# A two-layer decoder trunk on one Trainium2 core: identity transposes at the heads of groups left out, and the embedding input p laid out transposed by the host

## The chip, the core and the metric

The kernel runs on one core of a Trainium2 chip. The core has five engines, each with its own queue that it takes in order: TensorE (PE; its weight loads are listed as PEld), VectorE (DVE), ScalarE (ACT), GpSimd (POOL) and SyncE (SP), which here issues the DMAs. Engines wait for each other by semaphores. The metric is the device time of one launch in microseconds; three runs are known of the kernel before.

## The reference

The reference is a decoder trunk with two layers, on x of 256 rows and 1024 columns in float32. It computes, for layer i = 0, 1:

```
x = post_norm(x, 0.5 * swiglu(x, ffn1_w_in[i], ffn1_w_out[i]), ...)   # D_FF 2816
mix = fox_mixer(x, ...)  if i == 0  else  mla_mixer(x, ...)
x = post_norm(x, mix, ...)
x = post_norm(x, 0.5 * swiglu(x, ffn2_w_in[i], ffn2_w_out[i]), ...)
gate = sigmoid(x @ ple_w_gate[i] + ple_b_gate[i])
x = post_norm(x, gate * (p[i] @ ple_w_proj[i]), ...)                   # PLE_DIM 256
```

Here post_norm(x, d) is the layer norm of alpha * x + d. The FoX mixer is causal attention with 16 heads of 64 and a forget gate whose logarithms are summed along the sequence. The MLA mixer has 16 heads, a latent for the queries (384) and one for keys and values (256 + 64 rotary columns); the latter is computed once, from the x that leaves layer 0, by `kv_down`. p is an input of 2 x 1 x 256 x 256: a row of 256 for each layer and position.

## The kernel before

**Products.** Every matmul of the reference is computed as three products of operands that are split in a high and a low part: high x high, high x low, low x high (`mm3`, L608; `mm`, L615, records as L616). `parts` (L623) makes the two parts of an activation: ScalarE copies the source, rounded, to the high part (`high`, L629), and VectorE subtracts that from the source to get the low part (`low`, L633). x is held as two tiles of 128 rows, x0 and x1. `XT(t)` transposes one of them on TensorE, eight 128 x 128 blocks by a matmul with an identity (L620), into `xT`, in high and low parts.

**Weights.** A weight comes by a DMA of SP into one of three `raw` buffers, each 1 MB. ScalarE makes the high part of each half (L252, L260), VectorE the low part (L253, L264), into one of ten slots `hl0` to `hl9`, or into a tile that is free for the time (`fs`, `qk`, `ota`, `otb`, `gb`, `g4`). A raw buffer is loaded again when both its halves are split.

**The planner.** The class `Stream` decides at which point of the instruction stream a split is written. It keeps three model clocks while the kernel is built: one for TensorE (`pe_t`), one for ScalarE, one for VectorE. Each matmul adds to `pe_t` through `busy`, each transpose too:

```
def transpose(self, out, in_):
    self.nc.tensor.transpose(out, in_, self.ident)
    self.S.busy(pe=256)                                  # adds 116 ns to pe_t
...
if arrival <= self.pe_t + 500 and max(self.act_t, self.dve_t) <= self.pe_t + SLACK_NS:
```

`pump` (L384) is called after each group of products, and writes the next split when its load has arrived by the model and the two other clocks are no more than 1.6 us ahead of TensorE's. So what adds to `pe_t` decides ahead of which activation, norm or transposition a split stands in the queues of ScalarE and VectorE, and behind which a load on SP. The order of the splits among themselves is a written list (`ORDER`, and `FOX` in the mixer).

**The feed-forward network** (`ffn`, L721) runs over 11 chunks of 256 hidden columns. The first chunks are computed with the weights moving; the others in three groups, (2, 3, 4), (5, 6, 7), (8, 9, 10). At the head of each group, behind the first six matmuls of its first chunk, stands a `turn` on TensorE, which gets a free PSUM bank. In the first network of the program (`cold`) and in those that come before an embedding step (`ple`) the turns are:

- `T(0)` and `T(1)`: transposes of activations of the first chunks (not in the cold network);
- `spare` (L717): four transposes of the identity, whose result is not read;
- `ple_transpose` (L1033): four transposes of p, 128 x 128 each, and the parts of the result;
- `kv_transpose`: part of the key and value work, in the first network of layer 1.

**The embedding step** (`ple`, L1057) runs behind the second network of each layer. `ple_load` fetches p in the middle of that network (chunk 6), `ple_project` makes p @ Wp, and `ple` computes the gate with the slots of the weight `pg`: bias, eight weight tiles for x0, with `XT(1)` ahead of the seventh, then the same for x1 with `XT(0)` in that place, which transposes the normed x0 of the next layer. `post` is the sigmoid on ScalarE (L1080, with a table load ahead of the first), the product with the projection (L1081), the sum with x and its statistics (L689, L690); `ln_apply` is the norm (L698 to L705). Behind the boundary stand `kv_down`, whose weights are the four splits of 128 x 640, and the first chunk of the next network, whose silu is L783.

Of the kernel before, what the change touches and what calls it, by code (L numbers as in the profile page):

```python
# [510 lines left out]
class Trunk:  # L511
# [209 lines left out]
    def ffn(self, li, which, lni, kv=False, ple=False, at=None, cold=False, after=()):  # L721


        nc, S = self.nc, self.S
# [62 lines left out]
        def T(c):  # L787
            def f(tr):
                for t in range(2):
                    for kt in range(2):  # L790
                        self.transpose(
                            tr[:, 256 * kt + 128 * t : 256 * kt + 128 * t + 128],
                            g[c][:, 256 * t + 128 * kt : 256 * t + 128 * kt + 128],
                        )
                if c in summed:
                    gt = self.room(c, summed)
                    nc.scalar.activation(gt, tr, AF.Copy)
                    S.busy(act=512)
                    add(c)
                    return  # L800
                o = self.tl([128, 2, 512], F32R, "g4", 6)
                self.parts(o[:, 0, :], o[:, 1, :], tr)
                gT[c] = o

            return f

        def HT(c, gate, up, what=None):
            for half in range(2):
                ps = self.bank(*(up if half else gate))
                for u in range(2):  # L810
                    w = self.use(("wiu", li, which, c, 2 * half + u))
                    for kk, b in ((kk, b) for kk in range(4) for b in range(2)):
                        k = 4 * u + kk
                        if (half, k, b) == (0, 1, 0) and what:
                            what(self.bank(*up))
                        col = slice(256 * kk + 128 * b, 256 * kk + 128 * b + 128)
                        self.mm3(
                            ps[:, 256 * b : 256 * b + 256], lambda i: w[:, i, col], lambda i: self.xT[:, :, i, k, :],
                            (k, b) == (0, 0), (k, b) == (7, 1),
                        )  # L820
                if half == 0:
                    gt = self.room(c, summed)
                    nc.scalar.activation(gt, ps, AF.Silu)  # L823
                    S.busy(act=512)
            close(c, gt, ps)
# [14 lines left out]
        def add(c):  # L840

            tt, f = nc.vector.tensor_tensor, self.full[c]
            b = lambda i, n=1: f[:, 128 * i : 128 * (i + n)]
            tt(
                b(4, 2).rearrange("p (a b) -> p a b", b=128), b(0)[:, None, :].to_broadcast([128, 2, 128]),
                b(1, 2).rearrange("p (a b) -> p a b", b=128), op=ALU.subtract,
            )
            tt(b(6), b(5), b(1), op=ALU.subtract)
            tt(b(7), b(6), b(3), op=ALU.add)
            S.busy(dve=700)  # L850
            tag, o = self.home(homes)
            self.high(o[:, 0, :], f[:, 128:1024])
            S.between_sums()
            self.low(o[:, 0, :], o[:, 1, :], f[:, 128:1024])
            forms[c] = tag, o
# [93 lines left out]
        else:  # L949
# [14 lines left out]

        turns = (
            None if cold else T(0),
            self.spare if cold else T(1),
            self.kv_transpose if kv else self.ple_transpose if ple else self.spare,
        )
        x = self.turn["h"] if cold else 1 - self.turn["h"]  # L970
        for i, group in enumerate((((1,) + GROUPS[0]) if cold else GROUPS[0],) + GROUPS[1:]):
            for c in group:
                for f in at.get(c, ()):
                    f()
                if c == 2:
                    S.lend("gb")
                if c == 8:
                    S.reclaim("gb")
                if c == 10:
                    S.check("gb")  # L980
                    self.load_gb(li, lni)
                if c == 10 and kv:
                    self.kv_transpose_rope()
                if i == 0 and c == group[0]:
                    banks = ("tr", self.turn["tr"]), ("tr", 1 - self.turn["tr"])
                    turn = turns[0] and (lambda _: turns[0](self.bank("h", 1 - x)))
                    HT(c, *banks, turn)
                else:
                    HT(c, ("h", x), ("h", 1 - x), turns[i] if c == group[0] else None)
            if i < 2:  # L990
                if i == 1 and kv:
                    self.flush()
                sums([c for c in summed if (c < 5 and (cold or c != 1)) == (i == 0)], ("h", x))
                x = 1 - x
            if i == 1:
                S.lend(*after)
                combine()
# [26 lines left out]

    def ple_load(self, li):
        self.ple_p = self.tl([128, 512], F32, "g4", 6)
        for t in range(2):
            self.dma(
                self.ple_p[:, 256 * t : 256 * t + 256],
                None if self.rec else self.a["p"][li, 0, 128 * t : 128 * t + 128, :],  # L1030
            )

    def ple_transpose(self, tr):  # L1033
        nc = self.nc
        pt = self.ple_p
        for i in range(4):
            c = slice(128 * i, 128 * i + 128)
            self.transpose(tr[:, c], pt[:, c])
        self.ple_pT = self.tl([128, 2, 512], F32R, "g4", 6)
        self.parts(self.ple_pT[:, 0, :], self.ple_pT[:, 1, :], tr)  # L1040

    def ple_project(self, li):
        nc = self.nc
# [809 lines left out]
    Trunk(nc, (sb, ps), a, S, False, dr.tile([16, 256], F32, name="fox_c")).run()  # L1853


_INS = ["x", "p", "ln_g", "ln_b", "ple_b_gate", "fox_b_f", "mla_q_norm", "kv_norm"]


def _packed(np, a):

    def tiles(w, k):
        r, c = w.shape
        return w.reshape(r // (128 * k), k, 128, c).transpose(0, 2, 1, 3).reshape(r // (128 * k), 128, k * c)

    o = {}
    for n in ("ffn1", "ffn2"):
        w = a[n + "_w_in"].reshape(2, 2, 4, 128, 2, NCH, 256)
        o[n + "_in"] = w.transpose(0, 5, 1, 3, 2, 4, 6).reshape(2, NCH, 2, 128, 2048).copy()
        w = a[n + "_w_in"].reshape(2, 8, 128, 2, NCH, 256).transpose(0, 4, 3, 2, 1, 5).reshape(2, NCH, 2, 128, 2048)
        for li in range(2):  # L1870
            c = 1 if (n, li) == ("ffn1", 0) else 2
            o[n + "_in"][li, c:] = w[li, c:]
        o[n + "_out"] = np.stack([tiles(w, 2) for w in a[n + "_w_out"]])
    w = a["fox_w_in"][0]
    o["fq"], o["fk"] = (
        np.concatenate([tiles(w[:, c : c + 256], 8) for c in range(c0, c0 + 1024, 256)]) for c0 in (0, 1024)
    )
    o["fv"] = tiles(w[:, 2048:2560], 4)
    o["fvb"] = tiles(w[:, 2560:2816], 8)[0]
    o["fvc0"] = tiles(w[0:768, 2816:3088], 6)[0]  # L1880
    o["fvc1"] = tiles(w[768:1024, 2816:3088], 2)[0]
    o["fo"] = tiles(a["fox_w_o"][0], 2)
    o["mo"] = tiles(a["mla_w_o"][0], 2)
    o["pg"] = np.stack([tiles(w, 2) for w in a["ple_w_gate"]])
    o["pp"] = np.stack([tiles(w, 2) for w in a["ple_w_proj"]])
    o["kd"] = tiles(a["kv_w_down"], 4)
    o["dq"] = tiles(a["mla_w_dq"][0], 4)
    w = a["mla_w_uq"][0]
    r = w[:, :, 128:192].reshape(384, 1024)
    o["qr0"], o["qr1"] = tiles(r[0:256], 2)[0], tiles(r[256:384], 1)[0]  # L1890
    u = a["kv_w_up"]
    o["kvv"] = np.concatenate([tiles(u[:, h : h + 4, 128:256].reshape(256, 512), 2) for h in range(0, 16, 4)])
    n = np.concatenate([u[:, :, 0:128], w[:, :, 0:128]], 0)
    o["kq"] = np.concatenate([tiles(n[:, h : h + 2].reshape(640, 256), 5) for h in range(0, 16, 2)])
    t = a["x"][0].T.reshape(8, 128, 256)
    o["xt0"] = t[0:2]
    o["xt1"] = t[2:8].reshape(3, 2, 128, 256).transpose(0, 2, 1, 3).reshape(3, 128, 512)
    w = o["ffn1_in"][0, 0].reshape(2, 128, 4, 512).transpose(0, 2, 1, 3).reshape(8, 128, 512)
    o["w00"], o["w0"] = np.stack([w[0, :, 0:256], w[0, :, 256:512]]), w[1:8]
    return o  # L1900
# [34 lines left out]
```

## Time and profile before

| what | value |
|---|---|
| runs | 1050.86, 1048.7, 1050.29 us; median 1050.29 |
| profiled execution | 1049.6 us, span 1047.8 us, granted clock 0.998 |
| busy TensorE / weight loads | 1035.6 us (99%) / 948.6 us (91%) |
| busy VectorE / ScalarE / GpSimd | 891.8 us (85%) / 592.9 us (57%) / 58.0 us (6%) |
| DMA | 202.74 MB, mean 193 GB/s |

A row of a timeline gives the start in us from the span's start, the time from the first start to the last end of the instructions taken together, the engine, the line of the kernel, the operation, its output and inputs by the program's names, shapes, and the count; in square brackets the idle time of the engine before it and what ended that. A row of a group gives its summed busy time, the mean of one in ns, and idle time. The chain of waits is followed back from the last instruction of the program.

### The profile page before, as it was taken

Reading aid. Unit: us, or ns where it says so; the run is one execution under the profiler, and the core shown is the slowest. Engines: PE = TensorE matmul, PEld = TensorE weight load, DVE = VectorE, ACT = ScalarE, POOL = GpSimd, SP = SyncE. Lnnn points to the kernel's source line nnn. Section 1 sums busy time; section 2 is a strip of 40 time slices with the busy share of each in tenths; the row PEclk is TensorE's granted clock in tenths of the full one; section 3 lists DMA queues with packets and bytes.
Section 4 is the critical chain, followed back from the end, with each engine's and each line's share of the span. In section 5 each row is a group of like instructions: output and inputs, shape, how many; then the busy total and the mean of one; then the engine's idle time right before and its main releaser. Section 6 shows DMA issues by size and latency. Waiting matters only on the chain.

```text
span 1047.8 us, 17555 instructions
## 1 busy us (share of the span) xinstructions
PE 1035.6 (99%) x7085; PEld 948.6 (91%) x7085; DVE 891.8 (85%) x1312; ACT 592.9 (57%) x901; POOL 58.0 (6%) x88
## 2 busy tenths in 40 slices
PE   9999999999999999999999999999999999999996
PEld 8999898899889999998899898988999889898986
DVE  5788977868898979978979899888887989889877
ACT  6555563666755555663565646646776564646541
POOL 0000000122300000000220000000000000000000
PEclk9999999999999999999999999999999999999999
DMA  7855586455636363673674545743445564555732
GB/s 281 305 191 188 185 298 243 162 168 169 216 128 246 121 252 125 241 282 132 236 260 151 195 169 190 270 142 112 145 156 179 183 214 162 200 190 176 271 125 81
DMA packets 37476, 202.74 MB, mean 193 GB/s; under 512 B 3970, under 2 KB 9874, under 8 KB 16532
## 3 DMA queue, kind: packets, MB, share of 16 engines
q1 hardware_dynamic: 37396, 201.63, 54.3%
q8 instruction: 55, 0.90, 0.3%
q14 instruction: 25, 0.20, 0.1%
HBM read 200.55 MB, written 1.06 MB: 192 GB/s over the span
## 4 chain that ended last, share of the span: by engine, by line
PE 95%; DVE 2%; ACT 1%; issue 1%; DMA 0%; SPq 0%; DVEq 0%; ACTq 0%
PE h L616 53%; PE y L616 29%; PE tr L616 10%; PE tr L620 2%; DVE hl L253 1%; PE h L620 1%; DMA raw<-in_w_dram 0%; PE tr L1375 0%; DVE ts L300 0%; DVE x L705 0%; DVE tr L1720 0%; ACT qk L629 0%; DVE PT L633 0%; DVE ts L306 0%; DVE raw L308 0%
## 5 line engine op out<-in xcount | busy, mean ns | idle before, releaser
L616 PE MATMUL h<-xT,hl 128*128 128x256 f32 x3144 | 366.1, 277 | 1.2 <-ACT hl L327 0.7
L616 PEld LDWEIGHTS h<-xT,hl 128*128 128x128 f32 x3144 | 362.0, 188 | 2.9 <-ACT hl L327 1.2
L253 DVE TENSOR_TENSOR hl<-raw,hl 128x1024 fp32r<-128x1024 f32 (+5 forms) x271 | 314.2, 1190 | 36.1 <-ACT hl L252 35.0
L252 ACT ACTIVATE hl<-raw 128x1024 fp32r<-128x1024 f32 (+5 forms) x271 | 267.8, 1027 | 70.6 <-DVE raw L308 41.3
L616 PE MATMUL y<-hl,g 128*128 128x512 f32 x336 | 78.6, 391 | 0.0
L616 PEld LDWEIGHTS y<-hl,g 128*128 128x128 f32 x336 | 62.5, 188 | 12.6
L616 PE MATMUL h<-hl,xT 128*128 128x512 f32 (+2 forms) x312 | 67.9, 371 | 0.0
L616 PEld LDWEIGHTS h<-hl,xT 128*128 128x128 f32 x312 | 54.9, 188 | 9.8
L616 PE MATMUL y<-hl,otb 128*128 128x512 f32 x219 | 58.0, 399 | 0.0
L264 DVE TENSOR_TENSOR hl<-raw,hl 128x1024 fp32r<-128x1024 f32 (+2 forms) x44 | 52.3, 1192 | 0.8 <-ACT hl L260 0.7
L616 PE MATMUL y<-hl,xT 128*128 128x512 f32 (+3 forms) x282 | 52.7, 334 | 0.0
L260 ACT ACTIVATE hl<-raw 128x1024 fp32r<-128x1024 f32 (+2 forms) x44 | 45.2, 1029 | 9.7 <-DVE raw L308 9.1
L629 ACT ACTIVATE xT<-tr 128x512 fp32r<-128x512 f32 x28 | 16.1, 597 | 58.9 <-PE tr L620 58.9
L616 PEld LDWEIGHTS y<-hl,xT 128*128 128x128 f32 x282 | 44.1, 188 | 4.6 <-ACT xT L629 0.4
L616 PEld LDWEIGHTS y<-hl,otb 128*128 128x128 f32 x219 | 39.8, 188 | 8.4 <-DVE otb L633 0.3
L616 PE MATMUL y<-hl,ota 128*128 128x512 f32 x177 | 46.8, 398 | 0.1
L700 POOL TENSOR_TENSOR rs<-ve,mhalf 128x1 f32<-128x1 f32 x16 | 15.1, 942 | 519.8 <-DVE ve L699 519.8
L616 PE MATMUL tr<-xT,hl 128*128 128x256 f32 x360 | 42.5, 277 | 0.0
L616 PEld LDWEIGHTS tr<-xT,hl 128*128 128x128 f32 x360 | 41.7, 188 | 0.4
L616 PEld LDWEIGHTS y<-hl,ota 128*128 128x128 f32 x177 | 32.7, 189 | 7.7 <-DVE hl L253 0.6
L823 ACT ACTIVATE P<-h 128x512 f32<-128x512 f32 x33 | 19.7, 596 | 33.0 <-PE h L616 32.6
L300 DVE TENSOR_TENSOR ts<-raw 128x1024 f32<-128x1024 f32 x29 | 35.4, 1222 | 0.6
(322 smaller groups left out, 1632.7 us busy)
## 6 DMA issues: line engine op xcount, KB each, us to landing
raw<-in_ffn_in_dram SPq DMA_DIRECT2D x85, 1024.0 KB, 5.0
raw<-in_ffn_out_dram SPq DMA_DIRECT2D x44, 1024.0 KB, 5.0
raw<-in_pg_dram SPq DMA_DIRECT2D x8, 1024.0 KB, 4.9
raw<-in_mo_dram SPq DMA_DIRECT2D x8, 1024.0 KB, 4.8
raw<-in_kq_dram SPq DMA_DIRECT2D x8, 640.0 KB, 4.2
gb<-in_ln_g_dram SPq DMA_DIRECT2D x8, 512.0 KB, 5.9
gb<-in_ln_b_dram SPq DMA_DIRECT2D x8, 512.0 KB, 7.5
raw<-in_fk_dram SPq DMA_DIRECT2D x4, 1024.0 KB, 5.6
```

The costliest lines, as they stand in the source:

```text
L252: nc.scalar.activation(hi, src, AF.Copy)
L253: nc.vector.tensor_tensor(lo, src, hi.bitcast(F32), op=ALU.subtract)
L260: nc.scalar.activation(hi, src, AF.Copy)
L264: nc.vector.tensor_tensor(lo, src, hi.bitcast(F32), op=ALU.subtract)
L300: tt(s[:, 0:1024].rearrange("p (a b) -> p a b", b=512), r[:, 0:512][:, None, :].to_broadcast([128, 2, 512]), r[:, 512:1536].rearrange("p ( ...
L616: self.nc.tensor.matmul(out, lhsT, rhs, start=start, stop=stop)
L620: self.nc.tensor.transpose(out, in_, self.ident)
L629: self.nc.scalar.activation(hi, src, AF.Copy)
L700: nc.gpsimd.tensor_tensor(rs, ve, self.mhalf, op=ALU.pow)
L823: nc.scalar.activation(gt, ps, AF.Silu)
```

## The change

The turn `spare` at the heads of the second and third group is left out, and with it every other turn of four transposes that only serves p. The host lays p out transposed, in the form in which `ple_transpose` left it: 128 partitions of 512 values for each layer. `ple_load` fetches it with one DMA of 128 x 512 in place of two of 128 x 256, and its parts are made at the start of the third group, from SBUF. The `spare` at the very start of the program stays, as do `T(0)`, `T(1)` and `kv_transpose`. Sixteen transposes go: four at each of the second and third group of the cold network, four in the second network of each layer.

```diff
@@ ffn
         turns = (
             None if cold else T(0),
-            self.spare if cold else T(1),
-            self.kv_transpose if kv else self.ple_transpose if ple else self.spare,
+            None if cold else T(1),
+            self.kv_transpose if kv else None,
         )
...
+            if i == 2 and ple:
+                self.ple_parts()
             for c in group:
...
     def ple_load(self, li):
         self.ple_p = self.tl([128, 512], F32, "g4", 6)
-        for t in range(2):
-            self.dma(
-                self.ple_p[:, 256 * t : 256 * t + 256],
-                None if self.rec else self.a["p"][li, 0, 128 * t : 128 * t + 128, :],
-            )
-
-    def ple_transpose(self, tr):
-        nc = self.nc
-        pt = self.ple_p
-        for i in range(4):
-            c = slice(128 * i, 128 * i + 128)
-            self.transpose(tr[:, c], pt[:, c])
+        self.dma(self.ple_p, None if self.rec else self.a["pT"][li])
+
+    def ple_parts(self):
         self.ple_pT = self.tl([128, 2, 512], F32R, "g4", 6)
-        self.parts(self.ple_pT[:, 0, :], self.ple_pT[:, 1, :], tr)
+        self.parts(self.ple_pT[:, 0, :], self.ple_pT[:, 1, :], self.ple_p)
...
+    o["pT"] = a["p"][:, 0].reshape(2, 2, 128, 2, 128).transpose(0, 4, 1, 3, 2).reshape(2, 128, 512)
```

Lines behind L1035 count seven less in the changed kernel (L1081 is its L1074, L1448 its L1441).

The planner's clock of TensorE misses 16 x 116 ns, and a part of the splits is written at other points. On TensorE the order of what is left is the same. Three places at the boundary of the layers follow, the first on ScalarE, from the splits of the last two gate weights (`hl5`, `hl6`) to the sigmoids of x0, before and then in the changed kernel; `hl7`, `hl0`, `hl2` and `hl1` take the 128 x 640 splits of `kv_down`, and the xT rows are the high parts of x1.

```order
L252 ACTIVATE hl5_5222<-raw_5106 128x1024
L252 ACTIVATE hl6_5279<-raw_5106 128x1024
L252 ACTIVATE hl7_5290<-raw_5132 128x640
L252 ACTIVATE hl0_5296<-raw_5132 128x640
L629 ACTIVATE xT_75<-tr0_5301 128x512
L629 ACTIVATE xT_75<-tr1_5308 128x512
L252 ACTIVATE hl2_5321<-raw_5170 128x640
L252 ACTIVATE hl1_5327<-raw_5170 128x640
L1080 ACT_TABLE_LOAD
L1080 ACTIVATE g4_5336<-y3_5248 128x512
L1080 ACTIVATE g4_5336<-y0_5250 128x512
```

```order
L252 ACTIVATE hl5_5260<-raw_5090 128x1024
L252 ACTIVATE hl6_5269<-raw_5090 128x1024
L629 ACTIVATE xT_75<-tr0_5277 128x512
L629 ACTIVATE xT_75<-tr1_5284 128x512
L252 ACTIVATE hl7_5294<-raw_5119 128x640
L252 ACTIVATE hl0_5300<-raw_5119 128x640
L252 ACTIVATE hl2_5308<-raw_5154 128x640
L252 ACTIVATE hl1_5314<-raw_5154 128x640
L1073 ACT_TABLE_LOAD
L1073 ACTIVATE g4_5320<-y3_5229 128x512
L1073 ACTIVATE g4_5320<-y0_5231 128x512
```

All four splits of `kv_down` now stand behind the xT rows, between them and the table load; two of them stood ahead.

The second place is on VectorE, around the norm of x1 that ends the embedding step of layer 0; `otb` takes the last quarter of the first weight of the next network, and L1448 (now L1441) is a one-column row of `kv_down`.

```order
L253 TENSOR_TENSOR otb_5429<-raw_5299,otb_5429 128x1024
L1081 TENSOR_TENSOR g4_5438<-g4_5438,ota_5062 128x512
L689 SCALAR_TENSOR_TENSOR x1_70<-x1_70,g4_5438 128x512
L690 BN_STATS st4_5437<-x1_70 128x6
L1081 TENSOR_TENSOR g4_5438<-g4_5438,ota_5062 128x512
L689 SCALAR_TENSOR_TENSOR x1_70<-x1_70,g4_5438 128x512
L690 BN_STATS st4_5437<-x1_70 128x6
L698 BN_AGGR mv_5447<-st4_5437 128x2
L699 TENSOR_SCALAR ve_5448<-mv_5447 128x1
L705 SCALAR_TENSOR_TENSOR x1_70<-x1_70,mv_5447,gb_5240 128x512 x2
L705 SCALAR_TENSOR_TENSOR x1_70<-x1_70,rs_5449,gb_5240 128x512 x2
L1448 TENSOR_SCALAR ve_5485<-ss_5484 128x1
```

```order
L1074 TENSOR_TENSOR g4_5417<-g4_5417,ota_5040 128x512
L689 SCALAR_TENSOR_TENSOR x1_70<-x1_70,g4_5417 128x512
L690 BN_STATS st4_5416<-x1_70 128x6
L1074 TENSOR_TENSOR g4_5417<-g4_5417,ota_5040 128x512
L689 SCALAR_TENSOR_TENSOR x1_70<-x1_70,g4_5417 128x512
L690 BN_STATS st4_5416<-x1_70 128x6
L698 BN_AGGR mv_5426<-st4_5416 128x2
L699 TENSOR_SCALAR ve_5427<-mv_5426 128x1
L705 SCALAR_TENSOR_TENSOR x1_70<-x1_70,mv_5426,gb_5221 128x512 x2
L705 SCALAR_TENSOR_TENSOR x1_70<-x1_70,rs_5428,gb_5221 128x512 x2
L1441 TENSOR_SCALAR ve_5464<-ss_5463 128x1
L253 TENSOR_TENSOR otb_5491<-raw_5303,otb_5491 128x1024
```

The low part of `otb` stood ahead of x1's chain and now stands behind it and behind the one-column row.

The third place is on ScalarE, a little later: the high parts of the next network's first weights, the sigmoids of x1, two rows of `kv_down` (L1457, L1447), and the table load and silu of the first chunk (L783).

```order
L252 ACTIVATE hl3_5420<-raw_5299 128x1024
L252 ACTIVATE otb_5429<-raw_5299 128x1024
L1080 ACTIVATE g4_5438<-y1_5355 128x512
L1080 ACTIVATE g4_5438<-y2_5357 128x512
L1457 ACTIVATE PT_5247<-h0_5457 128x320
L1447 ACTIVATE PT_5247,ss_5484<-PT_5247 128x256
L252 ACTIVATE hl8_5512<-raw_5330 128x1024
L252 ACTIVATE hl5_5521<-raw_5330 128x1024
L783 ACT_TABLE_LOAD
L783 ACTIVATE P_5529<-h1_5483 128x256
```

```order
L252 ACTIVATE hl4_5399<-raw_5272 128x1024
L252 ACTIVATE hl3_5410<-raw_5303 128x1024
L1073 ACTIVATE g4_5417<-y1_5339 128x512
L1073 ACTIVATE g4_5417<-y2_5341 128x512
L1450 ACTIVATE PT_5228<-h0_5436 128x320
L1440 ACTIVATE PT_5228,ss_5463<-PT_5228 128x256
L252 ACTIVATE otb_5491<-raw_5303 128x1024
L252 ACTIVATE hl8_5502<-raw_5317 128x1024
L783 ACT_TABLE_LOAD
L783 ACTIVATE P_5508<-h1_5462 128x256
L252 ACTIVATE hl5_5516<-raw_5317 128x1024
```

The high part of `otb` has moved behind the rows of `kv_down`, and the one of `hl5`, the second weight of the next chunk, behind the silu.

2 lines of the change are left out of this document (1 added, 1 removed).

## The prediction

> **What bounds the kernel now.** I read the page first: the busy line and the first line of the chain that ended last.
>
> ```profile
> PE 1035.6 (99%) x7085; PEld 948.6 (91%) x7085; DVE 891.8 (85%) x1312; ACT 592.9 (57%) x901; POOL 58.0 (6%) x88
> PE 95%; DVE 2%; ACT 1%; issue 1%; DMA 0%; SPq 0%; DVEq 0%; ACTq 0%
> ```
>
> The reader is to see that TensorE is busy for 1035.6 of 1047.8 us and carries 95% of the chain. So an instruction that leaves TensorE's queue shortens the program by its own slot, and work on VectorE or ScalarE is free until it makes TensorE wait. VectorE at 85% has the least room: a split's lower half that comes one place later in its queue is the first thing that can turn into a wait. So I went to the timeline of TensorE at the four places where transposes go, and then, with the order of instructions before and after, to each place where a split has moved.
>
> **What the transposes cost.** The timeline of TensorE at the heads of the groups (start, busy time, instruction):
>
> ```profile
> 70.92 0.87 PE L616 MATMUL h<-xT,hl 128*128 128x256 f32 x6
> 71.63 0.60 PE L620 MATMUL h<-ident 128*128 128x128 f32 x4
> 71.98 2.30 PE L616 MATMUL h<-xT,hl 128*128 128x256 f32 x18
> 74.12 2.88 PE L616 MATMUL h<-xT,gb 128*128 128x256 f32 x24
> 76.84 2.43 PE L616 MATMUL h<-xT,hl 128*128 128x256 f32 x20
> ...
> 119.59 0.60 PE L620 MATMUL h<-ident 128*128 128x128 f32 x4
> ...
> 428.31 0.87 PE L616 MATMUL h<-xT,hl 128*128 128x256 f32 x6
> 429.16 0.66 PE L620 MATMUL h<-ident,g 128*128 128x128 f32 x4
> 429.57 0.60 PE L616 MATMUL h<-xT,hl 128*128 128x256 f32 x3
> ...
> 960.30 0.60 PE L620 MATMUL h<-ident,g 128*128 128x128 f32 x4
> ```
>
> The 24 matmuls of one weight half with four transposes among them take 74.12 - 70.92 = 3.20 us; the next 24 without any take 76.84 - 74.12 = 2.72. Four transposes therefore cost 0.48 us. All four fours read alike (0.60, 0.60, 0.66, 0.60), so the sum is 4 x 0.48 = 1.92. At 428.31 the six matmuls ahead of the transposes take 0.85 until the next start, where at 70.92 they take 0.71: the 0.14 between is a wait that goes with them. Together 2.06 us.
>
> The transposes' own duration is longer than their slot:
>
> ```profile
> L620 PE MATMUL h<-ident,g 128*128 128x128 f32 x20 | 3.1, 275 | 0.0
> ```
>
> One lasts 275 ns, and the slot is 0.48 / 4 = 0.12 us because the next one starts before it ends. The Trainium skill (TensorE: Matmul & The Clock Gate, Part 4: PE-mode transpose) gives about 275 ns for a transpose in a kernel, so by its price 16 would be worth an estimated 4.4 us. This trace agrees with the duration, but its starts decide against taking it as the price.
>
> What replaces them costs nothing that I can find. p comes by one DMA in place of two on the same SP queue. Its high part on ScalarE and low part on VectorE (each 128x512, as before) read SBUF in place of PSUM, and are issued at the head of the group in place of behind the transposes. The work that hides them is the group's own matmuls; without that cover they would cost one half of each L629 and L633 pair quoted for the boundary below, 1.09 / 2 + 1.28 / 2 = 1.2 us.
>
> **What moves.** The planner counts 16 x 116 ns less TensorE time, and from there emits some splits at other points. Most have microseconds to spare. At three places they do not.
>
> *First place, the start of the FoX mixer, a gain.* TensorE waits a little for x1's layer norm, and VectorE runs a split ahead of that norm, which the changed order puts behind it.
>
> ```profile
> 186.69 1.23 DVE L253 TENSOR_TENSOR hl<-raw,hl 128x1024 fp32r<-128x1024 f32 x1 [0.26 <-ACT hl L252]
> ...
> 192.23 1.41 DVE L705 SCALAR_TENSOR_TENSOR x<-x,rs,gb 128x512 f32<-128x512 f32 x2
> ...
> 193.08 0.63 PE L620 MATMUL tr<-ident,x 128*128 128x128 f32 x4 [0.33 <-issue]
> ```
>
> The norm comes 1.2 us earlier and the wait of 0.33 goes: a gain of 0.33 (bounds 0 and 0.4).
>
> *Second place, the end of the FoX mixer, a loss.* One split is deferred through the mixer and lands ahead of the low part of the probabilities of the third head group.
>
> ```profile
> 281.34 1.02 DVE L633 TENSOR_TENSOR PT<-tr,PT 128x512 fp32r<-128x512 f32 x2
> ...
> 282.41 1.22 PE L616 MATMUL h<-PT,g 128*128 128x512 f32 x6
> ```
>
> Those two low parts then end at about 281.34 + 1.02 + 1.2 = 283.5, and the product takes them from its third matmul of six (0.2 us each), about 282.9 for the first and 283.5 for the second. I take 0.3 (bounds 0 and the whole 1.2). The two places cancel.
>
> *Third place, the boundary of the layers, a loss, and the term that decides.* First ScalarE and VectorE around x0's last norm, then TensorE:
>
> ```profile
> 493.67 1.09 ACT L629 ACTIVATE xT<-tr 128x512 fp32r<-128x512 f32 x2 [6.10 <-PE tr L620]
> 494.64 1.37 ACT L252 ACTIVATE hl<-raw 128x640 fp32r<-128x640 f32 x2
> 496.03 1.28 ACT L1080 ACT_TABLE_LOAD   x1
> 497.32 1.09 ACT L1080 ACTIVATE g<-y 128x512 f32<-128x512 f32 x2
> ...
> 518.20 0.39 ACT L783 ACTIVATE P<-h 128x256 f32<-128x256 f32 x1 [1.34 <-PE h L616]
> 518.48 1.05 ACT L252 ACTIVATE hl<-raw 128x1024 fp32r<-128x1024 f32 x1
> ```
>
> ```profile
> 497.95 0.69 DVE L1081 TENSOR_TENSOR g<-g,ota 128x512 f32<-128x512 f32 x1 [0.33 <-ACT g L1080]
> ...
> 503.82 1.40 DVE L705 SCALAR_TENSOR_TENSOR x<-x,rs,gb 128x512 f32<-128x512 f32 x2
> 505.14 2.35 DVE L253 TENSOR_TENSOR hl<-raw,hl 128x1024 fp32r<-128x1024 f32 x2
> 507.41 1.28 DVE L633 TENSOR_TENSOR xT<-tr,xT 128x512 fp32r<-128x512 f32 x2
> 508.61 1.21 DVE L253 TENSOR_TENSOR hl<-raw,hl 128x1024 fp32r<-128x1024 f32 x1
> 509.75 1.21 DVE L253 TENSOR_TENSOR otb<-raw,otb 128x1024 fp32r<-128x1024 f32 x1
> 510.88 0.68 DVE L1081 TENSOR_TENSOR g<-g,ota 128x512 f32<-128x512 f32 x1
> ...
> 518.12 2.35 DVE L253 TENSOR_TENSOR hl<-raw,hl 128x1024 fp32r<-128x1024 f32 x2
> ```
>
> ```profile
> 503.98 1.52 PE L616 MATMUL y<-hl,xT 128*128 128x512 f32 x6
> 505.34 1.03 PE L620 MATMUL tr<-ident,x 128*128 128x128 f32 x8
> ...
> 516.61 1.55 PE L616 MATMUL h<-otb,xT 128*128 128x512 f32 x6
> 518.00 2.91 PE L616 MATMUL h<-hl,xT 128*128 128x512 f32 x12
> ```
>
> (a) In the changed order the first two down-projection splits (128x640) stand behind the xT pair, so four in place of two lie between 494.7 and the table load: 1.37 us more. The sigmoid g, which x0's chain waits for (0.33), ends as much later, and so does the chain: its last L705 pair at 505.22 + 1.37 = 506.59. TensorE's eight transposes of x0 start at 505.34; the first four need the first of the pair, the other four, due at about 505.8, the second. They wait 506.6 - 505.8 = about 0.85 (S1), with what is queued behind them: the last gate products and the down projection.
>
> (b) The low part of otb, until now at 509.75 ahead of x1's chain, stands behind that chain and its one-row L1448. VectorE's queue from 506.59: one split 1.13, the xT pair 1.20, two splits 2.27, x1's chain 518.12 - 510.88 = 7.24, otb's low part 1.21: 519.6. TensorE wants it in the third of otb's six matmuls, 516.61 + 0.46 = 517.07, so it is 2.55 late, of which S1 has been paid: S2 = 1.7. Without the delay in (a) it would still end at 518.3, 1.2 late.
>
> (c) ScalarE now makes the high part of the second weight of the next chunk (before 518.20) behind the silu of L783, which waits for the very chunk that otb ends. From that silu's start the high part is ready 0.28 + 1.05 later, at 519.53 on this scale; TensorE wants it after four matmuls, 518.00 + 0.92. S3 = 0.65.
>
> S1 + S2 + S3 = 3.2 us. TensorE has no idle time behind this to win it back. Bounds: 1.85 if (a) costs nothing, 3.9 if S1 is the whole 1.37; nothing at all if the chain from 497.95 to 509.75 is not as rigid as its gapless rows look.
>
> **The sum**, against the profiled execution's 1049.6: -2.06 for the transposes, -0.33 and +0.3 in the FoX mixer, +3.2 at the boundary: +1.1, so 1050.7 us. The profiled execution is 0.7 below the median of the three runs (1050.29), well inside their spread of 2.2, so I leave it there.
>
> **The rivals.**
> *The boundary keeps up: faster.* ScalarE idles 6.10 us ahead of 493.67, so a small shift of TensorE's arrival could let the splits through earlier than I think, and the gates' chain with it. Against it: both engines take their queues in order, and the order shows these splits behind a wait for TensorE. Price: 1049.6 - 2.06 - 0.03 = 1047.5.
> *The transposes are worth their whole duration: faster.* 16 x 0.275 = 4.4 in place of 1.92, against it the starts at 71.63 and 71.98. With the boundary as I have it: 1048.2. It is the price that the Trainium skill's figure above would give.
> *The loads fall behind: slower.* otb's buffer of raw weights comes free at 519.6 in place of 510.96, so the next load into it, and every load behind it on the one SP queue, is issued 8.6 us later, while TensorE is only 3.2 later. The ring is then 5.4 us behind.
>
> ```profile
> raw<-in_ffn_in_dram SPq DMA_DIRECT2D x85, 1024.0 KB, 5.0
> ```
>
> A load takes 5.0, so the first one lands at 524.6 and is split by 527; from the second group of the next FFN on it decides where a weight's lead is under 5.4. If half of this gap reaches TensorE, +2.7: 1053.4. Against it: the first use of the weight is, by the order, ten microseconds and more behind that.
> *The change does not do what it says* cannot be on TensorE, since the order shows the 16 transposes gone; only their slots could turn out to have been idle time, 1049.6 + 1.1 + 2.06 = 1052.8. The gapless starts around them speak against it.
>
> **Chances.** My sum, with S between its bounds (1049.3 to 1051.8): 0.46. The boundary keeps up: 0.27. Transposes at full duration: 0.04. Loads behind: 0.18. Slots idle: 0.05. Two thousandths, 2.1 us, is about what can be told from no change here. The first, the second, and a little of the low end make faster 0.31; the loads, most of the idle slots and the high end slower 0.26; the rest, 0.43, is the same. The range goes from just under the case in which the boundary keeps up to the loads' price: 1047.3 to 1053.4; the likeliest case alone spans 1049.3 to 1051.8.
>
> **What would show it.** In the changed profile, 24 matmuls at the head of those groups start 2.72 us ahead of the next weight half, as the others do. TensorE's waits list the transposes of x (L620) waiting for x at the boundary, then a matmul waiting for otb's low part (L253) for 1.2 to 2 us, then one for a high part from L252. The wait near 193 is gone. If the boundary shows no TensorE gap the time is about 1047.5 and steps (a) to (c) are wrong; if gaps show behind 530 with a DMA as releaser, the loads have fallen behind.

## The result, and the profile after

| kernel | runs | median (range), us | ratio to before, 95% interval |
|---|---|---|---|
| before, beside the changed kernel | 6 | 1050.26 | |
| changed | 6 | 1056.22 (1055.05 to 1058.77) | 1.0063 [1.0052, 1.0073] |

The change makes the kernel slower by 5.5 to 7.7 us. The forecast was 1050.7 and the range ended at 1053.4; the measured time lies beyond it. One launch of the kernel before and one of the kernel with two transposes took 3.7 ms; the ratios are without them. The profiled execution of the changed kernel took 1057.4 us, its span is 1055.7, 7.9 more than before. The busy line of its page:

```profile
PE 1042.3 (99%) x7069; PEld 953.9 (90%) x7069; DVE 892.4 (85%) x1312; ACT 592.9 (56%) x901; POOL 58.8 (6%) x88
```

TensorE has 16 instructions fewer and is busy for 6.7 us *more*. No new wait can do that: waits are not counted as busy. TensorE's waits (waited for, sum, times, longest) do show new ones:

```profile
PE h L616 <- DVE otb L253: 1.8, 1, 1.8
...
PE h L616 <- DVE PT L633: 0.6, 2, 0.4
...
PE tr L620 <- DVE x L705: 0.5, 1, 0.5
```

The waits for otb and for x are two of the three that the prediction named for the boundary; the third, for a high part from L252, is missing. The wait for PT is longer than before (0.6 in two, where it was 0.2 in one). No row of the list names a DMA.

To see where the 7.9 us arise I took the start of the same matmul in both traces. Where the changed kernel gains or loses:

| from the span's start, us | what is there | change, us |
|---|---|---|
| 0 to 9 | first weights arrive and are split | -1.06 |
| 9 to 71 | cold network, no edit ahead of it | +1.56 |
| 71.6, 119.6, 429, 960 | the four places of the transposes | -0.36, -0.35, -0.56, -0.36 |
| 72 to 119, 120 to 193, 430 to 465, 961 to 1000 | the matmuls behind these places | +0.92, +1.19, +1.04, +1.05 |
| 193, 282 | FoX mixer, both ends | -0.49, +0.65 |
| 505 to 520.07 | transposes of x0 wait (S1) | +0.87 |
| 520 to 528 | otb's low part waits; matmuls behind it | +1.9, +1.8 |

These are +7.9 with what is too small for a row. Two losses were not in the prediction: the matmuls *behind* the four places, 4.2 us, and those behind otb's wait. The first in the groups of TensorE's matmuls with 256 columns, in the stretches from 72 to 120 and from 120 to 193 us of the trace, each behind one place (busy time and mean ns of one), before:

```profile
L616 PE MATMUL h<-xT,hl 128*128 128x256 f32 x265 | 30.9, 277 | 0.0
...
L616 PE MATMUL h<-xT,hl 128*128 128x256 f32 x234 | 26.8, 276 | 0.0
```

and after:

```profile
L616 PE MATMUL h<-xT,hl 128*128 128x256 f32 x262 | 31.3, 281 | 0.0
...
L616 PE MATMUL h<-xT,hl 128*128 128x256 f32 x240 | 28.4, 281 | 0.0
```

The same matmul takes 281 ns in place of 276 or 277, and so it does behind the two later places (425 to 465 and 960 to 1000 us). The timeline at the first place shows what that means for the starts. After:

```profile
71.42 2.99 PE L616 MATMUL h<-xT,hl 128*128 128x256 f32 x24
74.24 2.99 PE L616 MATMUL h<-xT,gb 128*128 128x256 f32 x24
77.07 3.11 PE L616 MATMUL h<-xT,hl 128*128 128x256 f32 x25
```

24 matmuls take 74.24 - 71.42 = 2.82 us and 77.07 - 74.24 = 2.83, where before, behind the transposes, it was 2.72. By single starts the spacing is 117.8 ns in place of 113.3. Nothing waits, and no other spacing lasts: a run of these matmuls settles at the one or the other. 4.5 ns is nothing for one matmul, but behind each place there are 282 to 288 of them until the next stretch of other work, some 1.3 us (0.9 to 1.2 by the rows of the table), against the 0.48 that the prediction put down for four transposes. By these figures they pay from an estimated 0.48 / 0.0045 = 107 matmuls on.

At the boundary of the layers, TensorE after:

```profile
506.56 1.52 PE L616 MATMUL y<-hl,xT 128*128 128x512 f32 x6
508.54 1.29 PE L620 MATMUL tr<-ident,x 128*128 128x128 f32 x8 [0.46 <-DVE x L705]
509.58 3.00 PE L616 MATMUL y<-hl,xT 128*128 128x512 f32 x12
...
520.07 0.40 PE L616 MATMUL h<-otb,xT 128*128 128x512 f32 x1
```

and further on, with the runs drawn together from another window:

```profile
522.24 2.33 PE L616 MATMUL h<-otb,xT 128*128 128x512 f32 x5 [1.77 <-DVE otb L253]
524.37 3.77 PE L616 MATMUL h<-hl,xT 128*128 128x512 f32 x12
527.98 1.04 PE L620 MATMUL tr<-ident,x 128*128 128x128 f32 x8
```

S1 is (508.54 - 506.56) - (505.34 - 503.98) = 0.62 ahead of the eight transposes and (509.58 - 508.54) - (506.13 - 505.34) = 0.25 within them: 0.87. (506.13 is the start behind the transposes before, in the next rows.) The wait for otb's low part is 1.77. But then the matmuls themselves are slow. The twelve of the next weight take 527.98 - 524.37 = 3.61 us, where before they took 520.75 - 518.00 = 2.75, by the second of these rows of before:

```profile
506.13 3.00 PE L616 MATMUL y<-hl,xT 128*128 128x512 f32 x12
...
520.75 1.03 PE L620 MATMUL tr<-ident,x 128*128 128x128 f32 x8
```

The windows of the changed kernel (us, TensorE busy and instructions, granted clock, DMA share, GB/s) say why:

```profile
520.00:522.00 2.00, 0.47 (x3) 1.00 0.00 0
522.00:524.00 2.00, 1.76 (x5) 0.62 0.25 57
524.00:526.00 2.00, 2.00 (x7) 0.53 0.97 406
526.00:528.00 2.00, 2.00 (x10) 1.00 0.15 61
```

The granted clock is the share of the full clock that TensorE was given. Behind the wait it is 0.62 and 0.53 in these windows, which is one half for about 3.4 us: nine matmuls of 512 columns start 0.43 us apart, where 2.75 / 12 = 0.23 is usual. The third wait of the prediction, S3, does not show in this trace; the slow matmuls seem to give the splits time to catch up.

### The profile page after: what moved, and what is told of

Same layout as the page of the kernel before. It is cut to its first block, busy times and chain, and to the rows that moved or that the text cites. A ratio compares the mean times of both kernels' runs of the same rounds, so it can differ in the third digit from the quotient of the medians.

```text
span 1055.7 us, 17522 instructions
## 1 busy us (share of the span) xinstructions
PE 1042.3 (99%) x7069; PEld 953.9 (90%) x7069; DVE 892.4 (85%) x1312; ACT 592.9 (56%) x901; POOL 58.8 (6%) x88
## 3 DMA queue, kind: packets, MB, share of 16 engines
HBM read 200.55 MB, written 1.06 MB: 191 GB/s over the span
## 4 chain that ended last, share of the span: by engine, by line
PE 49%; DVE 2%; ACT 1%; issue 0%; DVEq 0%; ACTq 0%
PE h L616 26%; PE y L616 15%; PE tr L616 6%; PE tr L620 1%; DVE x L705 0%; PE h L620 0%; DVE hl L253 0%; DVE x L689 0%; DVE st L690 0%; DVE tr L1713 0%; ACT qk L629 0%; ACT hl L252 0%; DVE g L1074 0%; DVE otb L253 0%; ACT xT L1631 0%
## 5 line engine op out<-in xcount | busy, mean ns | idle before, releaser
L616 PE MATMUL h<-xT,hl 128*128 128x256 f32 x3144 | 370.6, 279 | 0.2 <-DVE hl L329 0.2
L616 PEld LDWEIGHTS h<-xT,hl 128*128 128x128 f32 x3144 | 367.5, 189 | 1.6 <-ACT xT L629 0.6
L253 DVE TENSOR_TENSOR hl<-raw,hl 128x1024 fp32r<-128x1024 f32 (+4 forms) x272 | 315.6, 1191 | 38.6 <-ACT hl L252 37.6
L252 ACT ACTIVATE hl<-raw 128x1024 fp32r<-128x1024 f32 (+4 forms) x272 | 268.8, 1026 | 67.8 <-DVE raw L308 41.2
```

Source lines behind the costliest of these rows:

```text
L252: nc.scalar.activation(hi, src, AF.Copy)
L253: nc.vector.tensor_tensor(lo, src, hi.bitcast(F32), op=ALU.subtract)
L616: self.nc.tensor.matmul(out, lhsT, rhs, start=start, stop=stop)
```

## The experiments

Two theories stood after the result. *Spacing*: the loss behind the four places comes from the missing transposes on TensorE. *Order*: all of it comes from the splits that stand elsewhere since the planner counts less, through something that the trace does not show as a wait. The kernel before ran beside each group of kernels, with medians from 1049.59 to 1049.69 us.

**Order kept, no transposes.** The planner counts four transposes at each place and none is issued; all splits stand as before. p comes laid out by the host.

```diff
+    def counted(self, n, ple):                  # n = 0 here
+        def f(tr):
+            for k in range(4):
+                if k < n:
+                    self.nc.tensor.transpose(tr[:, 128 * k : 128 * k + 128], self.ident, self.ident)
+                self.S.busy(pe=256)
+            if ple:
+                self.ple_parts()
...
-            self.spare if cold else T(1),
-            self.kv_transpose if kv else self.ple_transpose if ple else self.spare,
+            self.counted(n, False) if cold else T(1),
+            self.kv_transpose if kv else self.counted(n, ple),
```

> The 16 transposes are gone as in the change, but the planner still counts 16 x 116 ns, so every engine's order is that of the kernel before. Spacing theory: in the profiles a run of 128x256 matmuls starts every 113.3 ns behind four transposes and every 117.8 ns without; with about 330 matmuls at 70 to 125 us, 260 at 125 to 200, 260 at 425 to 475 and 260 at 955 to 1010 kept at the slower spacing, 1110 x 4.5 ns = +5.0, less 1.9 for the transposes' slots: +3.1, 1053.4 us. Order theory (all of the loss comes from the moved splits at the boundary of the layers): only the slots count, -2.1, 1048.2 us.

Measured: 1051.55 us (1049.72 to 1052.65, 12 runs), ratio 1.0016 [1.0008, 1.0025]: 1.7 us slower with less work and the old order. That speaks for spacing: by the transposes' slots alone it would have been 1.9 faster. TensorE at the boundary:

```profile
518.79 1.55 PE L616 MATMUL h<-otb,xT 128*128 128x512 f32 x6
520.17 2.91 PE L616 MATMUL h<-hl,xT 128*128 128x512 f32 x12
```

No wait there, and 1.38 us for otb's six matmuls, as before. The loss is less than the 3.1 expected. In the profile one of the four stretches went to the close spacing by itself, which is worth 1.2 us; whether the median owes its smaller loss to that is not shown. The groups between 72 and 119 and between 121 and 193 us:

```profile
L616 PE MATMUL h<-xT,hl 128*128 128x256 f32 x264 | 31.4, 281 | 0.0
...
L616 PE MATMUL h<-xT,hl 128*128 128x256 f32 x240 | 27.4, 276 | 0.0
```

**Order of the change, transposes back.** Four transposes of the identity at each place, which the planner does not count.

```diff
+    def quiet(self, tr):
+        for k in range(4):
+            self.nc.tensor.transpose(tr[:, 128 * k : 128 * k + 128], self.ident, self.ident)
...
-            None if cold else T(1),
-            self.kv_transpose if kv else None,
+            self.quiet if cold else T(1),
+            self.kv_transpose if kv else self.quiet,
```

> The order of all engines is that of the changed kernel, with p laid out by the host, but four identity transposes stand again at the four places on TensorE, without being counted by the planner. Spacing theory: the 128x256 matmuls run at 113.3 ns as before, and what is left is the boundary: waits of 0.8 and 1.9 us for x0's norm and otb's low part, and 1.9 us of matmuls at half rate behind the second wait, so 1050.3 + 4.6 = 1054.9 us, with the half rate visible. Order theory: all of the changed kernel's loss stays and the slots of 1.9 us come on top, 1058.1 us.

Measured: 1053.0 us (1052.48 to 1055.13, 6 runs), ratio 1.0034 [1.0021, 1.0048]. Spacing had expected 1054.9 with the half rate behind the wait, order 1058.1; the time is nearer to the first, and its profile shows no half rate. So 16 more instructions make the changed kernel some 3 us faster, and what is left, 2.2 to 5.0 us, is the order. The first place:

```profile
71.06 0.60 PE L719 MATMUL h<-ident 128*128 128x128 f32 x4
71.42 2.30 PE L616 MATMUL h<-xT,hl 128*128 128x256 f32 x18
73.55 2.88 PE L616 MATMUL h<-xT,gb 128*128 128x256 f32 x24
76.27 3.90 PE L616 MATMUL h<-xT,hl 128*128 128x256 f32 x33
```

76.27 - 73.55 = 2.72: the close spacing is back. The boundary, with S3 in the open and the clock full:

```profile
519.26 1.43 PE L616 MATMUL h<-otb,xT 128*128 128x512 f32 x5 [1.78 <-DVE otb L253]
520.53 1.08 PE L616 MATMUL h<-hl,xT 128*128 128x512 f32 x4
522.11 2.16 PE L616 MATMUL h<-hl,xT 128*128 128x512 f32 x8 [0.49 <-ACT hl L252]
```

```profile
521.00:523.00 2.00, 1.50 (x7) 1.00 0.90 365
```

The four matmuls from 520.53 take 1.58 until the next start in place of 0.92: S3 = 0.66. The wait for otb is as long as in the changed kernel, 1.78 to 1.77, but no slow clock follows, though the DMA traffic is nearly as dense (a share of 0.90, and 0.97 there).

**Only p's layout.** As the first experiment with n = 4: the order and the number of transposes as before.

> The kernel before in order and in number of transposes; only p comes transposed from the host by one DMA, and the four transposes in the second network of each layer take the identity. Both theories: 1050.3 us, within 0.7. If p's layout or its one DMA cost anything, it would be slower by that alone.

Measured: 1049.81 us (1048.56 to 1051.93), ratio 1.0001 [0.9992, 1.0011]. The layout and the one DMA cost and bring nothing that can be told, as predicted.

**How many transposes does it take?** The first experiment with n = 1, then n = 2, order as before.

> As the kernel with the order kept, but with one identity transpose in place of four at each of the four places. Spacing theory, if one transpose is enough to bring on the faster spacing: 12 slots of 0.12 us saved and nothing lost, 1050.3 - 1.4 = 1048.9 us; if it is not enough, near the kernel with none, 1053.4 + 0.5 = 1053.9 us. Order theory: 1050.3 - 1.5 = 1048.8 us, with the spacing as it is in the kernel before.

> Order of the kernel before, two identity transposes in place of four at each of the four places. One was enough at two places of four in its profile (71 and 960 us, not 120 and 429). If two are enough at all four: eight slots of 0.12 saved, 1.0 us below the kernel before; if at half of them only: -1.0 + 2.3 = +1.3.

Measured: one, 1050.89 us (1049.56 to 1053.91), 1.0014 [1.0003, 1.0025]; two, 1050.54 us, 1.0003 [0.9994, 1.0012]. In the profiles one transpose is followed by the close spacing at 71 and 960 and by the wide one at 119 and 429; two by the close one at 120 and 960, the wide one at 71 and 429. A middle result, neither none nor always. Two transposes at 71 us:

```profile
71.32 0.38 PE L729 MATMUL h<-ident 128*128 128x128 f32 x2
...
73.66 2.99 PE L616 MATMUL h<-xT,gb 128*128 128x256 f32 x24
76.49 1.69 PE L616 MATMUL h<-xT,hl 128*128 128x256 f32 x13
```

**Is it any four small instructions?** In place of the transposes four matmuls of 64 columns on a tile of ones, counted as transposes.

```diff
-            self.nc.tensor.transpose(tr[:, 128 * k : 128 * k + 128], self.ident, self.ident)
+            self.nc.tensor.matmul(tr[:, 64 * k : 64 * k + 64], self.ones, self.ones[:, 0:64], start=True, stop=True)
```

> Order of the kernel before; in place of the four transposes at each of the four places stand four matmuls of 64 columns on a tile of ones, whose result is not read. If any short pause in the run of 128x256 matmuls brings on the 113.3 ns spacing, this does it for about 0.06 us each in place of 0.12: 0.5 to 1.0 us below the kernel before. If it needs the transposes themselves, the spacing stays 117.8 at the four places: +3 us as with none.

Measured: 1052.41 us (1051.01 to 1053.23), ratio 1.0024 [1.0015, 1.0033]. All four stretches are wide. The first:

```profile
70.79 0.53 PE L733 MATMUL h<-ones 128*128 128x64 f32 x4
71.15 2.37 PE L616 MATMUL h<-xT,hl 128*128 128x256 f32 x18
73.36 2.99 PE L616 MATMUL h<-xT,gb 128*128 128x256 f32 x24
76.18 2.05 PE L616 MATMUL h<-xT,hl 128*128 128x256 f32 x16
```

So a break in the run is not enough. Whether it is the 128 columns, the transposition or the operand that matters, this does not tell.

**Does a fifth place pay?** Four more transposes at the head of the first group of the cold network, order as before.

```diff
-            None if cold else T(0),
+            (lambda tr: self.quiet(self.bank("y", 3))) if cold else T(0),
```

> The order of the kernel before, identity transposes at the same four places, and four more at a fifth: the head of the first group of the cold network, near 11 us. In the profiles so far the spacing between there and 70 us is 113.3 ns in some executions and 117.8 in others (excess 0.03 us in the kernel before and in the one with transposes uncounted, 1.4 to 2.1 in three others), with nothing in the program to tell them apart. Spacing theory: the fifth set makes it 113.3 each time; costs 0.48, gains 2.0 in about half of the executions, so the median is 0 to 1 us below the kernel before and the runs lie closer together. If four transposes do not set the spacing: +0.5 us and the same spread.

Measured: 1049.9 us (1048.94 to 1051.09), ratio 1.0003 [0.9994, 1.0012]: no gain in the median, though in the profile the spacing from 9 to 71 us is the close one. Ahead of 71 us the spacing differs from execution to execution of the same code, so there was not always something to win.

**Boundary order given back.** The second experiment, and at the start of layer 0's embedding step the planner counts 12 transposes that are not issued, so that the splits of the boundary stand as before, but for one low part (that of `hl5`).

```diff
+        for _ in range(0 if last else 12):
+            S.busy(pe=256)
         full = ((0, 512), (512, 1024))
         bias(0, full)
```

> As the kernel with four uncounted transposes at the four places, but the planner's clock gets the missing 12 x 116 ns at the start of the embedding step of layer 0, so that at the boundary of the layers the down-projection splits, otb and the next weights stand again where they stood before the change (only the seventh gate weight's low part stays behind x1's norm); the FoX mixer keeps the changed order. If the boundary is worth what its waits show (0.8 + 1.9 + 0.7 = 3.4 us): the uncounted kernel's 1053.0 less 3.4, 1049.6 us, which is the kernel before. If the changed order costs elsewhere: it stays above by that.

Measured: 1049.15 us (1048.74 to 1051.12), ratio 0.9996 [0.9988, 1.0005]. Against the second experiment that is 1053.0 - 1049.15 = 3.85 us for the order of a few splits at the boundary. TensorE there:

```profile
516.42 1.55 PE L616 MATMUL h<-otb,xT 128*128 128x512 f32 x6
517.81 2.91 PE L616 MATMUL h<-hl,xT 128*128 128x512 f32 x12
```

1.39 us from the one start to the next, as before, and no wait. The small waits for PT in the FoX mixer (0.6 in two) remain, as this edit leaves them. With the transposes and the boundary's order both back the time of before is back: the two causes are the whole effect, within the interval of about 1 us. This version is no faster than before either, within what can be told.

**The slow clock behind the wait.** The changed kernel again, with two more profiles, and the second experiment with VectorE work of no effect (the maximum of x1 with itself, 128x512) ahead of otb's low part, two or four times.

```diff
         def s1():
+            for _ in range(2 if t == 0 else 0):          # or 4
+                xs = self.x[1][:, 0:512]
+                nc.vector.tensor_tensor(xs, xs, xs, op=ALU.max)
```

> The changed kernel once more. Spacing theory: 128x256 matmuls at 117.8 ns from 71 to 200, 425 to 475 and 955 to 1010 us again, whatever it is ahead of 71; time 1055 to 1058. The wait of 1.9 us for otb is there again; if the half rate behind it falls by chance, it can be missing, and the time is then some 1.2 us less (1.9 us of half rate against the 0.7 us wait that it hides).

> The changed kernel a third time, for the profile: the same spacing; half rate behind otb's wait or not.

> As the kernel with four uncounted transposes, with two more VectorE operations of 128x512 (each about 0.6 us, a maximum of x1 with itself, which changes nothing) ahead of otb's low part: TensorE's wait there grows from 1.9 to 3.1 us. If the half rate needs a wait longer than some length between 1.9 and 3.1, it shows in every profile here, and the time is 1053.0 + 1.2 + about 1.3 = 1055.5; if it is unrelated to the wait, only the 1.2 us is added: 1054.2.

> The same with four such operations: the wait grows to 4.4 us. Half rate behind it: 1053.0 + 2.5 + about 1.3 = 1056.8; none: 1055.5.

The changed kernel measured 1056.12 us (1053.43 to 1057.71, 4 runs), and 1055.21 in the one other execution that was profiled. In the first of the two profiles the stretch behind 120 us ran at the close spacing, against the expectation; the other three were wide, and in the second profile all four. The first at the boundary:

```profile
520.41 1.43 PE L616 MATMUL h<-otb,xT 128*128 128x512 f32 x5 [1.77 <-DVE otb L253]
521.68 4.57 PE L616 MATMUL h<-hl,xT 128*128 128x512 f32 x12
```

and the second:

```profile
520.90 1.43 PE L616 MATMUL h<-otb,xT 128*128 128x512 f32 x5 [1.75 <-DVE otb L253]
...
523.76 2.14 PE L616 MATMUL h<-hl,xT 128*128 128x512 f32 x8 [0.51 <-ACT hl L252]
```

Same kernel, same wait: once the twelve matmuls last 4.57 us, once the clock stays full and S3 shows with 0.51. The longer waits measured 1057.38 us (1055.75 to 1059.19), ratio 1.0071 [1.0051, 1.0091], with a wait of 3.1; and 1058.33 us (1057.83 to 1058.97), ratio 1.0080 [1.0060, 1.0099], with 4.6. The first of them:

```profile
521.29 1.48 PE L616 MATMUL h<-otb,xT 128*128 128x512 f32 x5 [3.10 <-DVE otb L253]
522.57 4.54 PE L616 MATMUL h<-hl,xT 128*128 128x512 f32 x12
```

Windows of the second, from its wait on:

```profile
521.19:524.61 3.42, 0.64 (x3) 1.00 0.00 0
524.61:528.02 3.41, 3.41 (x10) 0.50 0.84 300
```

Both longer waits are followed by the slow clock, with the same order of the splits as in the second experiment, which fits TensorE's standing still as its cause. With 1.8 us it came in two of four profiles.

The traces also show what separates those two from the others. Within one trace the granted clock rises and falls only at times that lie whole multiples of 3.413 us apart. The changed kernel has three profiles: the one of the result is the first, the two above are the second and third. In the first the clock changes at 7.07, 522.48 and 525.89 us, and 522.48 - 7.07 = 515.41 = 151 x 3.413; the same holds in all 14 profiles. That cuts a trace into stretches of 3.41 us, which begin elsewhere in each execution. In the first the wait, from 520.47 to 522.24, lies whole in one stretch; in the third the end of a stretch, at 520.44, cuts the wait in two. The first:

```profile
519.07:522.48 3.41, 1.64 (x8) 1.00 0.00 0
522.48:525.89 3.41, 3.41 (x9) 0.50 0.67 255
```

and the third:

```profile
517.03:520.44 3.41, 2.12 (x10) 1.00 0.00 0
520.44:523.85 3.41, 2.44 (x10) 1.00 0.60 173
```

TensorE is idle for 3.41 - 1.64 = 1.77 us of one stretch in the first, and the next stretch runs at half rate. In the third no stretch has more than 3.41 - 2.12 = 1.29 us idle, and none is slow. The second profile goes with the first (1.77 us), the one of the second experiment (transposes back) with the third (at most 1.47 us); the longer waits leave 2.16 and 2.78 us in one stretch. Over all 14 profiles, every stretch at the full clock with 1.93 us idle or more was followed by half rate, and none with 1.72 or less; in between it went both ways (1.77 twice with it, 1.78 and 1.84 without). So it is chance, and not the edit, whether a wait of 1.77 us falls whole into one stretch: an estimated (3.41 - 1.77) / 3.41 = 48% of executions, if a stretch can begin anywhere.

The times with the longer waits are 1.5 to 1.9 us above what was expected even with the slow clock. In the two profiles the boundary itself costs 2.1 and 3.6 us more than in the second experiment, no more than expected (2.5 and 3.8). In each of them one set of four transposes failed to bring the close spacing (at 70.6 and at 429.6 us), 1.0 and 1.1 us. But the first of these executions is the fastest of its four, so this does not explain the median; that stays open.

## Why the prediction was wrong, step by step

**The transposes.** The step that failed is "Four transposes therefore cost 0.48 us", taken as what is saved without them. The slots do go: 0.36, 0.35, 0.56 and 0.36, together 1.63 of the 2.06. But the comparison behind it was of 24 matmuls with transposes and the next 24 *behind* them, which ran at 2.72 us per 24 because of the transposes. Without them these take 2.83. The trace of before held a hint that was passed over: at 70.92 the six matmuls ahead of the transposes take 71.63 - 70.92 = 0.71, 118 ns each, against 113 behind them. In the kernels with transposes at all places and at the other heads of groups (`T(0)`, `T(1)`, `kv_transpose`), the close spacing followed 76 of 78 sets of four, in seven profiles. In four profiles without any at the four places, 14 of 16 stretches were wide. The step's true size, with slots and spacing, is 2.6 us lost in the profiled execution (-1.63 + 4.2), not 2.06 gained. The further 1.56 us between 9 and 71 us in it are not from the edit: wide spacing costs there 1.4, 0.0 and 0.1 us in the three profiles of the changed kernel, and 2.0 in the one with only p's layout changed.

**The rivals.** "The transposes are worth their whole duration" falls with the same rows. "The loads fall behind" (0.18) falls: no wait of TensorE names a DMA, and from 528 to 960 us the changed kernel's lag stays at 7.2 us. "The boundary keeps up" (0.27) falls with the waits above. "Slots idle" falls too: the slots were real, and went. None of the rivals was that removed instructions could slow the ones behind them.

**The FoX mixer.** The gain at its start was predicted as 0.33 and is 0.49, the loss at its end 0.3 and is 0.65. The mechanisms stand, but for one reading: the product waits for PT ahead of its second matmul and not its third. The two now cost 0.16 in place of nothing.

**The boundary.** S1 0.85, measured 0.87. S2 1.7, measured 1.94 with the wait of 1.8. S3 0.65, measured 0.66 where the clock stays full. Their sum is 3.5 to the predicted 3.2 (with small delays behind the waits the whole boundary costs 3.75 in that profile), and the order given back is worth 3.85 in medians. Steps (a) to (c) are right, read from the order of instructions and the queue times alone. Two slips in their sums change nothing: the times in (c) give 519.53 - 518.92 = 0.61 and not 0.65, and with S1 at 1.37 the three make 3.7 and not 3.9, so that the likeliest case would have ended at 1051.2 and not at 1051.8. VectorE started otb's low part at 520.97:

```profile
507.65 1.41 DVE L705 SCALAR_TENSOR_TENSOR x<-x,rs,gb 128x512 f32<-128x512 f32 x2
...
520.97 1.22 DVE L253 TENSOR_TENSOR otb<-raw,otb 128x1024 fp32r<-128x1024 f32 x1
```

13.3 us behind the norm, by the queue's sum in (b) 519.6 - 1.21 - (506.59 - 1.40) = 13.2.

What was missing there is the clock: behind the wait what follows may run at half rate for 3.41 us. In the profiles of the changed kernel with it the boundary loses 4.6 us, without it 3.7: some 0.9 more, with S3 hidden in it. Whether an execution has it is chance, by the stretches above. The claim "TensorE has no idle time behind this to win it back" is true, and it lost more than the waits.

**Together:** 1.1 predicted, and about 6.6 measured. The order alone (second experiment) costs 3.6 and the transposes' absence alone (first) 1.7, by their ratios. The 1.3 left over is of the size of the slow clock (0.9), which the second experiment's profile lacks, and of the one stretch that went close by itself in the first (1.2); which of them it is in the median was not settled.

## What to carry to other kernels

An instruction whose result nobody reads can still pay: price a removal by the pace of what stands *behind* it, first start to first start over the whole stretch, and look for two paces of one shape in the trace before summing slots. An engine's busy time that rises with fewer instructions means that a shape has changed its pace, or that the clock was lower for a while; the mean duration by stretch (276 or 281 ns here) finds it at once. In a program whose order follows a model clock, a removal of 0.1 us per instruction can move a split past a chain of microseconds; the order of both programs, laid beside the queue's times, foretold those waits to a few tenths.

## What the runs showed of the hardware

- **Two paces of the same matmuls.** Runs of 128x256 matmuls, each with its weight load, start every 113.3 or every 117.8 ns and stay there for hundreds. Behind stretches of 512 columns they mostly begin at 118 (at 14 of 18 places of the profile before). Four transposes bring on the closer pace nearly always, one or two sometimes, four matmuls of 64 columns in none of four places. By the Trainium skill (TensorE: Matmul & The Clock Gate, "Wait — 56ns, not 53.3ns?") a matmul back to back with another starts N / 2.4 + 2.5 ns later, an estimated 109 ns for 256 columns. Here each matmul comes with a weight load, and neither pace is that. Why transposes shift it, why they failed twice, and what sets the pace ahead of 71 us stay open.
- **Half rate after less than two microseconds.** The granted clock fell to one half for 3.41 us after a wait of 1.8 us in two of four profiles, and after 3.1 and 4.6 us in both. The Trainium skill (TensorE: Matmul & The Clock Gate, Part 1, "What's actually happening") tells of half rate after an idle window of about 3.4 us. The idle time needed was less here, and the measurement decides; that about one such window passes before the full rate comes back agrees with the 3.41 us. In these traces the clock changes only at the ends of stretches of 3.413 us, and 1.93 us or more of idle time in one stretch always brought half rate in the next, 1.72 or less never. Why 1.77 did twice and 1.84 did not is not known.
- **A matmul of 64 columns took no less time than a transpose of 128.** The four of 64 columns, each with its own weights of 128 x 128, hold TensorE for 71.15 - 70.79 = 0.36 us until the next start, and four transposes of 128 columns for 71.42 - 71.06 = 0.36.
